# The first quarter of the up projection: half products in a written order, the transposes of h2's last two row tiles at fixed places

## The chip, the cores and the metric

The kernel runs on one core of a Trainium2 chip. The metric is device time in microseconds (us). One execution is also recorded by the hardware profiler, and its trace shows every instruction of every engine: TensorE (PE, and PEld for its weight loads), VectorE (DVE), ScalarE (ACT), GpSimd (POOL) and SyncE (SP), which issues most loads.

## The reference

One decoder block on x of 512 tokens by 1024 features, float32. The change lies where the second half of the block begins:

```python
x = x + (merged @ w_out[l]).astype(x.dtype)
h2 = rmsnorm(x, norm_mlp_g[l])
z = jnp.square(jax.nn.relu(h2 @ w_up[l]))      # 1024 -> 4096
x = x + (z @ w_down[l]).astype(x.dtype)        # 4096 -> 1024
```

Ahead of it stand the input projection, differential attention, pooling and the gates; behind it the final norm.

## The kernel before

**Splitting.** Every float32 operand of a product is split in two parts in a narrower format: a rounded copy made by ACT ("hi") and the remainder made by DVE ("lo"). A product is hi*hi + hi*lo + lo*hi, so three matmuls stand for one. Weights are split by `split_w` (lines 110 to 114: the cast on line 112, the remainder on line 113).

**Seven products instead of eight.** The MLP is cut into four quarters of 1024 hidden features (`for q in range(4): up(q); down(q)`). In `up(q)` the matrix h2 is cut in 2 by 2 blocks (token halves of 256 by feature halves of 512), the weights likewise, and the product is formed with seven block products (a Strassen-like scheme) named by the form of h2 that they use: A11, A12 and A22 are blocks of h2 itself, S1 to S4 are sums and differences of blocks. In the first quarter their order is A11, A12, S1, S2, S3, A22, S4.

**One product** (`product`, lines 749 to 772) has two banks of the accumulation memory (i = 0, 1), and each bank two halves (p = 0, 1) of 256 columns. Such a half product is 12 matmuls of 256 columns: four times hi*hi (line 759) and hi*lo (line 761) in turn, then four times lo*hi (line 764). The two banks are two tiles. S2, S3 and A22 reuse A11's banks, S4 reuses S1's, so they wait until the earlier result has been taken out: by ACT copies (`keep`, line 776) or by DVE sums (`join`, line 780).

**h2 and its transposes** (lines 614 to 646). h2 is made in four row tiles of 128 tokens: DVE scales a row tile (line 623), TensorE transposes it in 2 banks of four 128 x 128 blocks (line 629), and ACT and DVE take the blocks out: for row tiles 0 and 1 as hi and lo of A11 and A12 (lines 641 and 642) and as a plain copy (line 646); for row tiles 2 and 3 as the sums that the S forms need (lines 634 and 635, and `forms_h2`, up to line 603) and as A22's hi and lo. So A11 and A12 need row tiles 0 and 1 alone; S1 is the first that needs row tiles 2 and 3. Row tiles 0 and 2 use accumulation banks 0 and 1, row tiles 1 and 3 use 2 and 3.

**Down** (`down`, line 828 on) takes the seven forms of z; its matmuls (lines 838, 840 and 841) are 512 wide. Its first product in the first quarter uses z's form A11, which is ready before `up` has ended.

**What sets the order.** Each engine runs its own instructions in one fixed order. That order isn't written out in the code: the framework's planner lays it out when the program is built, on a timeline that it simulates. `after(later, earlier)` adds an edge, that "later" is placed behind "earlier"; on one engine this is order alone and adds no wait. Matmuls into one bank keep their order; matmuls into different banks may be laid out in any order that the planner finds. Before the change there were two such edges in the first quarter: the first closing matmul of A11's last half product comes after the very last transpose (lines 765 and 766), and S4's very first matmul after A22's last (lines 768 to 771).

Of the kernel before, what the change touches and what calls it, by code (L numbers as in the profile page):

```python
# [51 lines left out]
def block_kernel(ctx, tc, xT, x_tok, gains, pos, consts, w_in, w_v, w_pool, w_out, w_up, w_dn, out):  # L52
# [4 lines left out]
    def after(later, earlier):  # L57
        tc.add_manual_dep(
            later.ins, earlier.ins.name,
            mybir.DependencyInfo(mybir.DependencyClass.NoSync, mybir.DependencyReason.DATA), reason="issue order",  # L60
        )

    state = {}
# [8 lines left out]
    def bank(i, name):  # L72
        return ps.tile([P, S], F32, tag=f"b{i}", name=name)
# [16 lines left out]
    def f(ap):  # L90
        return ap.bitcast(F32)
# [125 lines left out]
    for n in range(2):  # L217
        accs = [bank((0, 1, 2, 3, 4, 5, 6, 0)[4 * n + t], f"v{n}_{t}") for t in range(NT)]
        for kk in range(4):
# [7 lines left out]
            for k2 in range(2):  # L227
# [4 lines left out]
                k = 2 * kk + k2  # L232
# [11 lines left out]
            if n == 0 and 0 < kk < 3:  # L244
                i = kk - 1
# [287 lines left out]
    A11, A12, A22, A21, S1, S2, S3, S4 = range(8)  # L533
# [44 lines left out]
    def mm_rows(a_, t, k, w, start, stop):  # L578
        hi, lo = w
        sl, tsl = slice((k % 2) * 512, (k % 2) * 512 + 512), slice(t * P, t * P + P)  # L580
        T.matmul(a_, lhsT=mh[:, k, tsl], rhs=hi[:, sl], start=start, stop=False)
        T.matmul(a_, lhsT=mh[:, k, tsl], rhs=lo[:, sl], start=False, stop=False)
        T.matmul(a_, lhsT=ml[:, k, tsl], rhs=hi[:, sl], start=False, stop=stop)

    def x1_add(t, n, a_):
        xs = x1[:, t, n * 512 : n * 512 + 512]
        V.tensor_tensor(out=xs, in0=a_, in1=xs, op=ALU.add)
        square(t, n, R[t][:, 0:2, :].rearrange("p a t -> p (a t)"))
# [29 lines left out]
    for t in range(NT):  # L618
        a_ = bank(4 + t, f"po1_{t}")
        for k in range(NK):  # L620
            mm_rows(a_, t, k, ws[k // 2], k == 0, k == NK - 1)
        x1_add(t, 1, a_)
        V.scalar_tensor_tensor(out=h2[:, t % 2], in0=x1[:, t, :], scalar=row_scale(t, 1), in1=g2b, op0=ALU.mult, op1=ALU.mult)
        pv = []
        for b in range(2):
            pt = bank((t % 2) * 2 + b, f"h2T{t}_{b}")
            for j in range(4):
                k = 4 * b + j
                state["h2T"] = T.transpose(out=pt[:, j * P : j * P + P], in_=h2[:, t % 2, k * P : k * P + P], identity=ident)
            pv.append(pt.rearrange("p (j q) -> p j q", q=P))  # L630
        sl = slice((t % 2) * P, (t % 2) * P + P)
        if t > 1:

            A.copy(out=hw[:, 1, :, sl], in_=pv[0])
            V.tensor_tensor(out=hw[:, 0, :, sl], in0=pv[1], in1=hw[:, 1, :, sl], op=ALU.subtract)
            forms_h2((S1, S2), sl)
        if t == 3:
            forms_h2((S3,), slice(0, HS))
        for b in range(t // 2, 2):
            hi, lo = (gab[b][:, t // 2, i, :, sl] for i in range(2))  # L640
            A.copy(out=hi, in_=pv[b])
            part = V.tensor_tensor(out=lo, in0=pv[b], in1=f(hi), op=ALU.subtract)
            if t == 3:
                after(part, state[S3])
            if t < 2:
                A.copy(out=h2f[:, b, :, sl], in_=pv[b])
# [79 lines left out]
    def bank_view(pa):  # L726
        return [pa[i].rearrange("p (a t) -> p a t", a=2) for i in range(2)]
# [17 lines left out]
    def up(q):  # L745

        W = weights(w_up, q, "u", (A11, A12, S1, S2, S3, A22, S4) if q == 0 else (A11, S1, S2, S3, A22, A12, S4))

        def product(form, name, onto=None):
            w, pa = next(W), onto or [acc(f"u{name}{q}_{i}") for i in range(2)]  # L750
            rh, rl = gf[form]
            first.append(None)
            for i in range(2):
                hi, lo = w[i]
                for p in range(2):
                    a_ = pa[i][:, p * HS : p * HS + HS]
                    for k in range(4):
                        c = slice((p * 4 + k) * P, (p * 4 + k) * P + P)
                        m = T.matmul(a_, lhsT=hi[:, c], rhs=rh[:, k, :], start=p + k == 0 and onto is None, stop=False, skip_group_check=True)  # L759
                        first[-1] = first[-1] or m  # L760
                        T.matmul(a_, lhsT=hi[:, c], rhs=rl[:, k, :], start=False, stop=False, skip_group_check=True)  # L761
                    for k in range(4):
                        c = slice((p * 4 + k) * P, (p * 4 + k) * P + P)
                        m = T.matmul(a_, lhsT=lo[:, c], rhs=rh[:, k, :], start=False, stop=k == 3, skip_group_check=True)  # L764
                        if q == 0 and form == A11 and i + p == 2 and k == 0:
                            after(m, state["h2T"])

            if form == A22:
                state["m4"] = m
            elif form == S4:  # L770
                after(first[-1], state["m4"])
            return pa

        def keep(pa, r):
            for a_, r_ in zip(bank_view(pa), halves(r)):
                A.copy(out=r_, in_=a_)  # L776

        def join(pa, r):
            for a_, r_ in zip(bank_view(pa), halves(r)):
                V.tensor_tensor(out=r_, in0=a_, in1=r_, op=ALU.add)  # L780

        def z_of(r, sign, pa=None):
            for i, r_ in enumerate(halves(r)):
                A.activation(out=r_, in_=bank_view(pa)[i] if pa else r_, func=AF.Relu, scale=sign)
                ins = A.activation(out=r_, in_=r_, func=AF.Square)
            return ins

        ma = product(A11, "m1")
        keep(ma, R[0])
        if q == 0:  # L790
            forms_h2((S4,), slice(0, HS))

        def first_block():
            join(product(A12, "m2"), R[0])
            z_of(R[0], 1.0)
            if q > 0:
                zsplit(q, A11, R[0])

        if q == 0:
            first_block()  # L800
        mc = product(S1, "m5")
        keep(mc, R[2])
        product(S2, "m6", onto=ma)
        keep(ma, R[1])
        product(S3, "m7", onto=ma)
        join(ma, R[2])
        z_of(R[2], -1.0)
        product(A22, "m4", onto=ma)
        if q == 0:
            zsplit(q, A11, R[0])  # L810
        zhi["z21"] = z_of(R[3], 1.0, ma)
        sub(4, 2, 3)
        zsplit(q, S1, R[4])
        if q > 0:
            first_block()
        product(S4, "m3", onto=mc)
        join(mc, R[1])
        z_of(R[1], -1.0)
        zsplit(q, A12, R[1])
        sub(4, 4, 0, neg=True)  # L820
        zsplit(q, S2, R[4])
        sub(1, 4, 1, neg=True)
        zsplit(q, S4, R[1])
        sub(0, 0, 3)
        zsplit(q, S3, R[0])
        zsplit(q, A22, R[2])
# [166 lines left out]
```

## Time and profile before

| | us |
|---|---|
| three runs | 676.32, 676.32, 677.84 |
| median | 676.32 |
| span of the profiled execution, first to last instruction | 675.2 |
| its difference to the median, outside the span | 1.1 |
| TensorE's busy time in that span | 665.3 |
| first matmul of the up projection | 349.82 |
| last closing matmul of S3 begins its group of four | 382.21 |

The profile's times count from the first instruction of the span. A row of the timeline has the start, the length, the engine, the line in the kernel, the operation, the tiles (output, then inputs), the form and how many instructions are merged; in square brackets stands idle time of the engine ahead of it and what ended it. Matmul ends are modelled, so distances are best read from start to start. `um` are the accumulators of the up projection, `dm` those of down; `gab` holds h2's blocks A11, A12 and A22, `gss` the S forms; `wh` and `wl` are the parts of the weights, with the letters u and d for up and down.

### The profile page before, as it was taken

The page shows a single profiled execution, that of the slowest core. Times are in us where ns is not written, and L with a number is a line of the kernel's source. Part 1 is how long each engine was busy: PE and PEld are TensorE (multiplying, and loading weights), DVE is VectorE, ACT ScalarE, POOL GpSimd, SP SyncE. Part 2 cuts the span into 40 slices and gives each one's busy share as a digit, 9 for nine tenths or more (in the row PEclk, how much of TensorE's full clock was granted, in tenths as well). Part 3 has the DMA queues.
Part 4 walks back from the last instruction along what each step waited for, and adds up shares of the span by engine and source line. Part 5 has one row for each costly group of instructions (what it writes and reads, how often), then busy time and mean ns, then how long its engine had stood idle before and what let it go on. Part 6 is the DMA issues. An engine that isn't in the chain of part 4 may idle for free.

```text
span 675.2 us, 9995 instructions
## 1 busy us (share of the span) xinstructions
PE 665.3 (99%) x3686; PEld 579.9 (86%) x3686; DVE 529.1 (78%) x879; ACT 462.5 (68%) x741; POOL 123.0 (18%) x137
## 2 busy tenths in 40 slices
PE   9999999999999999999999999999999999999995
PEld 7788888888888888888889988899889998899884
DVE  6955877799979986975478989667994599747995
ACT  8465587978887698883477975367753696356874
POOL 6201110132133212520201020202103021210120
PEclk9999999999999999999999999999999999999999
DMA  8526574435254364574964678676969579493863
GB/s 272 189 71 182 126 152 125 102 94 126 87 139 105 101 171 94 126 193 177 309 194 79 196 172 241 153 179 155 234 190 197 200 156 260 125 213 131 213 125 124
DMA packets 32880, 109.34 MB, mean 162 GB/s; under 512 B 4032, under 2 KB 4928, under 8 KB 32832
## 3 DMA queue, kind: packets, MB, share of 16 engines
q0 software_dynamic: 10656, 38.80, 32.4%
q1 hardware_dynamic: 21744, 69.38, 29.0%
q8 instruction: 29, 0.48, 0.3%
q10 hardware_dynamic: 432, 0.52, 0.2%
q14 instruction: 19, 0.16, 0.1%
HBM read 106.59 MB, written 2.10 MB: 161 GB/s over the span
## 4 chain that ended last, share of the span: by engine, by line
PE 86%; DMA 5%; issue 5%; DVE 1%; ACT 1%; SPq 0%; DVEq 0%; POOLq 0%
PE dm L838 7%; PE dm L840 7%; PE dm L841 7%; PE um L759 7%; PE um L764 7%; PE um L761 7%; DMA wga_uNone<-w_up 5%; PE o L417 2%; PE ga L132 2%; PE ga L131 2%; PE gp L135 2%; PE k L132 2%; PE gp L132 2%; PE gp L131 2%; PE k L131 2%
## 5 line engine op out<-in xcount | busy, mean ns | idle before, releaser
L840 PE MATMUL dm<-wh_dt,z 128*128 128x512 f32 (+1 forms) x128 | 49.5, 387 | 0.0
L841 PE MATMUL dm<-wl_dt,z 128*128 128x512 f32 (+1 forms) x128 | 49.4, 386 | 0.0
L838 PE MATMUL dm<-wh_dt,z 128*128 128x512 f32 (+1 forms) x128 | 49.0, 387 | 0.0
L759 PE MATMUL um<-gss,wh_ut 128*128 128x256 f32 x192 | 48.1, 284 | 0.1
L761 PE MATMUL um<-gss,wh_ut 128*128 128x256 f32 x192 | 48.1, 283 | 0.0
L400 ACT ACTIVATE p<-p,st 128x128 f32<-128x128 f32 (+3 forms) x64 | 35.8, 560 | 14.1 <-DVE st L396 13.8
L112 ACT CAST wh_ut<-wga_uNone 128x1024 fp32r<-128x1024 f32 x24 | 24.9, 1053 | 28.8 <-PE dm L840 19.2
L856 DVE TENSOR_TENSOR x<-x,dm 128x512 f32<-128x512 f32 x48 | 32.8, 687 | 14.1 <-PE dm L841 14.0
L670 POOL DMA_DIRECT2D wga_dNone<-w_dn x16 | 14.2, 887 | 151.8 <-DVE wl_dt L113 151.8
L113 DVE TENSOR_TENSOR wl_ut<-wga_uNone,wh_ut 128x1024 fp32r<-128x1024 f32 x24 | 29.0, 1224 | 12.5 <-ACT wh_ut L112 12.5
L112 ACT CAST wh_ub<-wr_u 128x1024 fp32r<-128x1024 f32 x24 | 25.1, 1051 | 19.0 <-PE um L761 10.1
L670 POOL DMA_DIRECT2D wga_uNone<-w_up x18 | 15.6, 867 | 120.9 <-DVE wl_ut L113 86.9
L840 PE MATMUL dm<-wh_db,z 128*128 128x512 f32 x96 | 37.2, 389 | 0.0
L841 PE MATMUL dm<-wl_db,z 128*128 128x512 f32 x96 | 37.2, 389 | 0.0
L759 PEld LDWEIGHTS um<-gss,wh_ut 128*128 128x128 f32 x192 | 36.8, 192 | 0.3 <-ACT rawz L776 0.3
L761 PEld LDWEIGHTS um<-gss,wh_ut 128*128 128x128 f32 x192 | 36.9, 192 | 0.0
L838 PE MATMUL dm<-wh_db,z 128*128 128x512 f32 x96 | 35.8, 390 | 0.0
L113 DVE TENSOR_TENSOR wl_ub<-wr_u,wh_ub 128x1024 fp32r<-128x1024 f32 x24 | 29.2, 1222 | 7.9 <-ACT wh_ub L112 7.9
L112 ACT CAST wh_dt<-wga_dNone 128x1024 fp32r<-128x1024 f32 x24 | 24.8, 1050 | 14.6 <-issue 4.1
L735 DVE TENSOR_TENSOR z<-rawz,z 128x1024 fp32r<-128x1024 f32 x28 | 33.7, 1225 | 0.9 <-ACT z L732 0.9
L396 DVE CUSTOM_DVE_ANT_0 p<-s,mask 128x128 f32<-128x128 f32 (+3 forms) x64 | 30.3, 485 | 3.4 <-PE s L395 3.3
L732 ACT CAST z<-rawz 128x1024 fp32r<-128x1024 f32 x28 | 28.7, 1048 | 6.0 <-DVE rawz L741 4.9
(324 smaller groups left out, 2222.9 us busy)
## 6 DMA issues: line engine op xcount, KB each, us to landing
wr_u<-w_up SPq DMA_DIRECT2D x24, 512.0 KB, 5.3
wr_d<-w_dn SPq DMA_DIRECT2D x24, 512.0 KB, 4.2
wga_uNone<-w_up POOLq DMA_DIRECT2D x18, 512.0 KB, 6.7
wga_dNone<-w_dn POOLq DMA_DIRECT2D x16, 512.0 KB, 5.8
wr_k<-w_in SPq DMA_DIRECT2D x8, 512.0 KB, 3.3
wr_ga<-w_in SPq DMA_DIRECT2D x8, 512.0 KB, 3.3
wr_gp<-w_in SPq DMA_DIRECT2D x8, 512.0 KB, 4.2
wl_ga<-w_in POOLq DMA_DIRECT2D x8, 512.0 KB, 5.5
```

Source lines behind the costliest of these rows:

```text
L112: ins = A.copy(out=hi[:, sl], in_=raw[:, sl])
L113: (eng or G).tensor_tensor(out=lo[:, sl], in0=raw[:, sl], in1=f(hi)[:, sl], op=ALU.subtract)
L131: T.matmul(acc, lhsT=hi[:, c], rhs=rh[:, k, :], start=k == 0, stop=False)
L132: T.matmul(acc, lhsT=hi[:, c], rhs=rl[k], start=False, stop=False)
L400: A.activation(out=pr[:, c, :N], in_=pr[:, c, :N], func=AF.Exp, scale=-1.0, bias=st[:, c : c + 1], accum_out=st[:, 2 + c : 3 + c])
L735: V.tensor_tensor(out=z[:, 1], in0=r, in1=f(z[:, 0]), op=ALU.subtract)
L759: m = T.matmul(a_, lhsT=hi[:, c], rhs=rh[:, k, :], start=p + k == 0 and onto is None, stop=False, skip_group_check=True)
L761: T.matmul(a_, lhsT=hi[:, c], rhs=rl[:, k, :], start=False, stop=False, skip_group_check=True)
L764: m = T.matmul(a_, lhsT=lo[:, c], rhs=rh[:, k, :], start=False, stop=k == 3, skip_group_check=True)
L838: m = T.matmul(a_, lhsT=zh, rhs=hi[:, sl], start=p == 0 and start, stop=False, skip_group_check=True)
L840: T.matmul(a_, lhsT=zl, rhs=hi[:, sl], start=False, stop=False, skip_group_check=True)
L841: end = T.matmul(a_, lhsT=zh, rhs=lo[:, sl], start=False, stop=p == 3, skip_group_check=True)
```

## The change

Only the order on TensorE is changed, by edges in the first quarter; no instruction is added or taken away.

- The first transpose of every bank of every row tile is remembered (`state["h2T", t, b]`).
- In the first quarter every half product's first matmul is placed behind the last matmul of the half product before it in program order, through all seven products (`state["um"]`).
- Row tile 2's transposes are placed behind A11's second half product (i = 0, p = 1), row tile 3's behind A12's second half product.
- The edge to the very last transpose moves from A11's last half product to A12's third (i = 1, p = 0).

```diff
             for j in range(4):
                 k = 4 * b + j
+                if j == 1:
+                    state["h2T", t, b] = state["h2T"]
                 state["h2T"] = T.transpose(out=pt[:, j * P : j * P + P], in_=h2[:, t % 2, k * P : k * P + P], identity=ident)
...
                 for p in range(2):
+                    begin = None
                     a_ = pa[i][:, p * HS : p * HS + HS]
...
                         first[-1] = first[-1] or m
+                        begin = begin or m
...
                         m = T.matmul(a_, lhsT=lo[:, c], rhs=rh[:, k, :], start=False, stop=k == 3, skip_group_check=True)
-                        if q == 0 and form == A11 and i + p == 2 and k == 0:
+                        if q == 0 and form == A12 and (i, p, k) == (1, 0, 0):
                             after(m, state["h2T"])
+                    if q == 0:
+                        if (form, i, p) == (A11, 0, 1):
+                            for b in range(2):
+                                after(state["h2T", 2, b], m)
+                        elif (form, i, p) == (A12, 0, 1):
+                            for b in range(2):
+                                after(state["h2T", 3, b], m)
+                        if form != A11 or i + p:
+                            after(begin, state["um"])
+                        state["um"] = m
```

## The prediction

> **What bounds the kernel now.** I read the page first, then the busy time by stretches, then TensorE's timeline in the two stretches that stood out, and last the queues of ScalarE (ACT) and VectorE (DVE) beside them.
>
> ```profile
> span 675.2 us, 9995 instructions
> PE 665.3 (99%) x3686; PEld 579.9 (86%) x3686; DVE 529.1 (78%) x879; ACT 462.5 (68%) x741; POOL 123.0 (18%) x137
> ```
>
> TensorE is the bound. A matmul it doesn't issue in time is paid in full, provided that nothing behind it waits anyway. The stretches show where that holds (columns: length, then the busy time of PE, PEld, DVE, ACT, POOL, and the granted clock):
>
> ```profile
> 349.80:351.80 2.00, 1.42 (x8) 0.90 (x8) 2.00 (x5) 1.61 (x4) 0.00 (x0) 1.00 0.98 387
> 351.80:364.40 12.60, 12.60 (x108) 12.60 (x107) 10.76 (x16) 9.58 (x19) 1.73 (x2) 1.00 0.30 57
> 364.40:378.70 14.30, 14.30 (x121) 14.30 (x120) 12.59 (x13) 12.85 (x17) 1.73 (x2) 1.00 0.84 193
> 378.70:379.75 1.05, 0.64 (x4) 0.24 (x3) 1.05 (x2) 1.05 (x3) 0.00 (x0) 1.00 0.90 339
> 379.75:388.30 8.55, 8.55 (x71) 8.55 (x72) 8.55 (x9) 7.08 (x10) 0.00 (x0) 1.00 0.36 120
> 388.30:426.90 38.60, 38.60 (x195) 32.77 (x194) 35.95 (x37) 24.35 (x28) 5.25 (x6) 1.00 0.74 187
> 426.90:666.00 239.10, 239.10 (x1534) 218.80 (x1533) 183.69 (x202) 149.70 (x191) 33.26 (x38) 1.00 0.72 181
> ```
>
> From 351.80 us to the last matmuls TensorE stands still once, near 379 us. The quarter that is changed (349.8 to about 396 us) has two holes, and behind it lie 239.10 us without one. So whatever the change gains or loses in this quarter goes one to one into the time, as long as nothing new goes wrong behind it. The holes, by starts, since the ends of matmuls are modelled:
>
> ```profile
> 349.82 0.87 PE L759 MATMUL um<-gab,wh_ub 128*128 128x256 f32 x3
> 351.28 0.66 PE L629 MATMUL h2T<-ident,h 128*128 128x128 f32 x4 [0.58 <-ACT h2f L646]
> 351.80 0.39 PE L761 MATMUL um<-gab,wh_ub 128*128 128x256 f32 x1
> 352.02 0.28 PE L759 MATMUL um<-gab,wh_ub 128*128 128x256 f32 x1
> 352.14 0.28 PE L761 MATMUL um<-gab,wh_ub 128*128 128x256 f32 x1
> 359.89 1.03 PE L629 MATMUL h2T<-ident,h 128*128 128x128 f32 x8
> 360.69 0.96 PE L764 MATMUL um<-gab,wl_ub 128*128 128x256 f32 x6
> 364.35 0.40 PE L759 MATMUL um<-gss,wh_ut 128*128 128x256 f32 x2
> ...
> 378.39 0.52 PE L764 MATMUL um<-gss,wl_ut 128*128 128x256 f32 x3
> 379.24 0.38 PE L759 MATMUL um<-gss,wh_ub 128*128 128x256 f32 x1 [0.32 <-ACT gss L602]
> 379.71 0.39 PE L759 MATMUL um<-gss,wh_ut 128*128 128x256 f32 x1
> ```
>
> In the stream a 256-wide matmul starts every 0.12 us (352.02 to 352.14), so a half product of 12 is 1.44 us. Eight transposes hold TensorE from 359.89 to 360.69, some 0.10 us each. Just after a hole the first matmul takes 0.22 us instead of 0.12 (351.80 to 352.02), so a hole costs 0.10 us on top.
>
> **First hole, A11's beginning.** The three L759 at 349.82 are first matmuls of three banks: a half product alternates L759 and L761, and three L759 in a row can't be of one. A11's next matmul is the L761 at 351.80, which multiplies by the remainder of h2's first two row tiles. Who makes that remainder:
>
> ```profile
> 348.66 1.28 DVE L623 SCALAR_TENSOR_TENSOR h<-x,st,rawz 128x1024 f32<-128x1024 f32 x1
> 349.86 1.88 DVE L642 TENSOR_TENSOR gab<-h2T,gab 128x512 fp32r<-128x512 f32 x3
> 355.91 1.28 DVE L623 SCALAR_TENSOR_TENSOR h<-x,st,rawz 128x1024 f32<-128x1024 f32 x1
> 361.18 0.69 DVE L635 TENSOR_TENSOR hw<-h2T,hw 128x512 f32<-128x512 f32 x1
> 362.58 0.69 DVE L603 TENSOR_TENSOR gss<-hw,gss 128x512 fp32r<-128x512 f32 x1
> ```
>
> The third L642 ends at 349.86 + 1.88 = 351.74, and the L761 starts 0.06 us later. Program order of lines 638 to 642 makes that third one row tile 1's first bank, which A11 needs. So A11 waits for DVE until 351.80 whatever TensorE's order is. Before, two first matmuls of other banks (2 x 0.12) and the four transposes of row tile 2's first bank (4 x 0.10, from 351.28) were done inside this wait. The change holds the first matmul of each half behind the last of the half ahead, and row tile 2's transposes behind A11's second half. Nothing else of TensorE's is ready then, so this cover is gone: 0.24 + 0.40 = **+0.64 us**. Bounds: nothing, if DVE takes the remainders ahead of the 1.28 us of scaling row tile 2 (which is less urgent now, but was ready first); nor can it cost more, since the wait's end is DVE's.
>
> A rule of the Trainium skill bears on this ("TensorE: Matmul & The Clock Gate", Part 2, Step-by-step): weight loads may be pulled ahead, but the matmuls stay in program order. In the trace nothing passes the transposes that wait until 351.28, which agrees. By that rule a written order turns each late operand into a hole; if matmuls could pass each other, this term would be nothing and the sum below 0.64 us lower.
>
> **Row tiles 2 and 3.** No transpose is added. Row tile 2 goes behind A11's second half, which costs only what stands above. Row tile 3's eight stood behind all of A11 and A12's first bank except 6 closing matmuls (the x6 at 360.69), and stand now behind all of that: 6 x 0.12 = 0.72 us later, and with the 0.64 us they start at about 361.3 instead of 359.9. Behind them wait ACT L634 (in the fence below), DVE L635 and the two steps of S1's form, ending with DVE L603 at 362.58 + 0.69 = 363.27. That moves to about 364.6. S1 started at 364.35 and would now start at 364.35 + 0.64 = 365.0. So 0.4 us of margin is left: cost nothing. If DVE puts one weight remainder of 1.22 us (L113's size, below) ahead of it, it is 0.8 us late, and with the 0.10 that makes 0.9 us: the upper bound.
>
> **Second hole, the middle of S3.** After the last of S3's first bank (378.39 + 3 x 0.12 = 378.75) came a first matmul of S4, taken ahead of its turn, at 379.24, and S3's second bank only at 379.71. ACT's queue beside it:
>
> ```profile
> 360.53 0.59 ACT L634 COPY hw<-h2T 128x512 f32<-128x512 f32 x1 [1.48 <-PE h2T L629]
> 375.04 2.24 ACT L112 CAST wh_ut<-wga_uNone 128x1024 fp32r<-128x1024 f32 x2
> 377.18 1.05 ACT L112 CAST wh_ub<-wr_u 128x1024 fp32r<-128x1024 f32 x1
> 378.14 1.04 ACT L602 CAST gss<-hw 128x1024 fp32r<-128x1024 f32 x1
> 379.09 0.57 ACT L776 COPY rawz<-um 128x512 f32<-128x512 f32 x1
> ```
>
> The S4 matmul waited for L602 (ends 379.18), S3's second bank for L776, the copy that frees its bank, which ends at 379.66. The chain forbids the S4 matmul there (it opens S4's second bank), but that alone frees nothing: the copy is ACT's. Lost before: 0.96 us less the 0.12 of useful work, plus 0.10: 0.94 us. After, TensorE comes to this place 0.64 us later, at 379.39. If ACT's queue stands as it is, 379.71 - 379.39 + 0.10 = 0.42 us is still lost, a saving of **0.52 us**. If ACT runs earlier by 0.3 us (row tile 2's copies leave a place ahead of the S1 casts), the whole 0.94 us is saved; if ACT is late by as much as TensorE, nothing. I take the rows as they stand.
>
> **A22 and S4.** S4's second bank ran between A22's two banks and can't any more:
>
> ```profile
> 382.69 0.28 PE L759 MATMUL um<-gab,wh_ut 128*128 128x256 f32 x1
> 385.57 0.28 PE L761 MATMUL um<-gss,wh_ub 128*128 128x256 f32 x1
> 388.33 0.40 PE L838 MATMUL dm<-wh_db,z 128*128 128x512 f32 x1
> 388.56 0.40 PE L840 MATMUL dm<-wh_db,z 128*128 128x512 f32 x1
> ...
> 384.68 1.22 DVE L113 TENSOR_TENSOR wl_db<-wr_d,wh_db 128x1024 fp32r<-128x1024 f32 x1
> 385.81 0.69 DVE L780 TENSOR_TENSOR rawz<-um,rawz 128x512 f32<-128x512 f32 x1
> 386.42 1.22 DVE L700 TENSOR_TENSOR wga_dNone<-wr_d,wal_d 128x1024 f32<-128x1024 f32 x1
> ```
>
> A22's first bank ends at 385.57. Its second needs the join L780, which frees the bank at 385.81 + 0.69 = 386.50. In between only the down projection's first product is free. Its matmuls take 0.23 us (388.33 to 388.56); the first that needs a weight remainder is the third, at 385.57 + 0.46 = 386.03, and that remainder (L113) is done at 385.90. Before, the planner put down matmuls in this very place while A22 waited (388.33), so I take them as the cover: cost **nothing**. Without it A22 starts at about 386.55: 0.98 + 0.10 = 1.08 us. Below nothing it can't go, for this place had no hole.
>
> **The sum.** 0.64 - 0.52 = +0.12 us on a span of 675.2. The median of the runs shown, 676.32, lies 1.1 us over this execution's span; the same 1.1 us gives 675.2 + 0.12 + 1.1 = 676.4. What the measurement of this kernel tells from no change is about 0.3%, 2.0 us. The sum lies far inside it, and so do most of its bounds: -0.30 with ACT early, up to 0.12 + 0.9 + 1.08 = 2.1 with S1 late and A22 uncovered.
>
> **Rivals.**
>
> *Slower: A22 locked behind its join.* The place is 385.57 us. With S4 behind the chain, TensorE has only the down projection's matmuls there. DVE has no idle time in that stretch (8.55 of 8.55), and the planner lays its queue out anew. If two of the 1.22 us instructions slip ahead of L780, each taking 1.13 us of the queue (384.68 to 385.81), the join ends at 386.50 + 2.26 = 388.8. Without down matmuls in between, TensorE waits 3.2 us + 0.10, and the sum is +3.4: 679.7. It decides the sign once the uncovered wait passes 1.8 us, so from a join that ends after 387.4. Against it: the down product's first half was ready in just that place. For it: S4's second bank was the main cover before, 2.76 us of it (385.57 to 388.33), and it is gone. Chance 0.10.
>
> *Faster: both holes close.* DVE takes the remainders ahead of L623, A11 starts 1.2 us earlier and TensorE stands 0.6 us instead of 1.9; and ACT's copy comes early enough for S3. Then the first term becomes 0.64 - 1.2 = -0.56 and the second -0.94: -1.5, 674.8, still inside 0.3%. Only with a further gain behind it (the last hole's remainder, 0.6 us) does it reach -2.1: 674.2. Against it: L623's input was there first, and nothing of the change reaches DVE before 351 us. Chance of passing 2.0 us: 0.05.
>
> *The reshuffle.* The planner may change the order of ACT, DVE and the loads all through the later quarters. They have no hole now (239.10 of 239.10), so a new order can only leave that so or cost something. Casts of 1.05 us and remainders of 1.22 us are the units: one late costs about 1 us (677.4), two or more pass the bound. Chance of one 0.15, of passing the bound 0.03.
>
> *It does nothing.* The order changes only inside waits for DVE and ACT, so time stays: 676.3. This is inside the forecast's own range.
>
> **How the numbers follow.** The forecast with its own bounds has 0.67: 675.9 to 677.4 (with one of the two upper terms at most). With the one-late-cast case (677.4, 0.15) that makes 0.82 inside 675.4 to 678.0, which I give as the range: half a microsecond wider than these cases on each side, for the spread of the runs' median. Faster by over 0.3%: 0.05. Slower by over 0.3%: 0.10 + 0.03 = 0.13. Within: 0.82.
>
> **What would show it.** Right: in the changed profile TensorE has a hole of about 1.9 us behind A11's first matmul, ended by DVE L642, with no transpose in it; eight transposes in one row after 24 and after 72 matmuls of A11 and A12; no S4 matmul before A22's last; a hole of 0 to 0.4 us in the middle of S3, ended by ACT L776; down matmuls between A22's two banks. Wrong: A11's second matmul earlier than DVE's third L642 before it, a hole over 1.8 us at A22's second bank, S1 waiting for DVE L603, or new holes after the first quarter.

## The result and the profile after

The kernel after takes 679.27 us in the median (677.35 to 681.41, 16 executions), the kernel before 676.81 (676.02 to 678.71, 16 executions) beside it: a ratio of 1.0034 [1.0026, 1.0042]. The change makes the kernel slower by 2.5 us, a little more than the 0.3% that was given as the bound (which lies inside the interval). The forecast was 676.4, and its range ended at 678.0.

The page of the kernel after, the two rows that answer to those of before:

```profile
span 675.0 us, 9994 instructions
PE 664.4 (98%) x3686; PEld 580.0 (86%) x3686; DVE 528.9 (78%) x879; ACT 461.1 (68%) x741; POOL 122.7 (18%) x137
```

This span is no longer than that of before (675.2). So the span of one execution doesn't show the loss. The profiled execution of after took 677.35 us, the lowest of its 16. The loss has to be looked for in the stretches, and in the other executions. The busy time by stretches, kernel after (columns as in the prediction):

```profile
349.16:351.12 1.96, 0.39 (x3) 0.19 (x2) 1.96 (x5) 1.59 (x4) 0.00 (x0) 1.00 1.01 393
351.12:363.64 12.52, 12.52 (x106) 12.52 (x107) 9.69 (x15) 9.21 (x19) 1.72 (x2) 1.00 0.48 90
363.64:378.00 14.36, 14.36 (x122) 14.36 (x121) 13.93 (x15) 13.41 (x19) 1.73 (x2) 1.00 0.69 171
378.00:384.50 6.50, 6.50 (x56) 6.45 (x54) 6.50 (x7) 5.10 (x8) 0.00 (x0) 1.00 0.35 125
384.50:385.32 0.82, 0.16 (x3) 0.01 (x1) 0.82 (x3) 0.82 (x2) 0.00 (x0) 1.00 0.00 0
385.32:394.00 8.68, 8.68 (x72) 8.68 (x73) 8.25 (x8) 7.25 (x12) 3.51 (x4) 1.00 0.79 189
426.70:665.90 239.20, 239.20 (x1535) 218.87 (x1534) 182.60 (x200) 149.55 (x191) 33.18 (x38) 1.00 0.72 180
```

There are two holes, as before, but the second has moved: the stretch around 379 us is filled (6.50 of 6.50), and a new hole stands at 384.50 to 385.32. The later quarters are full, as before. TensorE's timeline of the kernel after at these places:

```profile
349.16 0.39 PE L762 MATMUL um<-gab,wh_ub 128*128 128x256 f32 x1
351.12 0.38 PE L765 MATMUL um<-gab,wh_ub 128*128 128x256 f32 x1 [1.57 <-DVE gab L644]
...
353.98 1.04 PE L631 MATMUL h2T<-ident,h 128*128 128x128 f32 x8
360.60 1.03 PE L631 MATMUL h2T<-ident,h 128*128 128x128 f32 x8
364.34 0.28 PE L762 MATMUL um<-gss,wh_ut 128*128 128x256 f32 x1
...
378.74 0.28 PE L762 MATMUL um<-gss,wh_ut 128*128 128x256 f32 x1
...
384.02 0.64 PE L768 MATMUL um<-gab,wl_ut 128*128 128x256 f32 x4
385.32 0.39 PE L762 MATMUL um<-gab,wh_ut 128*128 128x256 f32 x1 [0.66 <-DVE rawz L794]
...
394.06 0.40 PE L852 MATMUL dm<-wh_db,z 128*128 128x512 f32 x1
426.72 0.28 PE L762 MATMUL um<-gab,wh_ub 128*128 128x256 f32 x1
```

(L762, L765 and L768 were L759, L761 and L764 before, L631 was L629, L644 was L642, L790 was L776, L794 was L780, L798 was L784.) From A11's first matmul to the second quarter's first I count what I call *the quarter*: 426.72 - 349.16 = 77.56 us. Before it was 426.87 - 349.82 = 77.05, by this row of the kernel before:

```profile
426.87 0.28 PE L759 MATMUL um<-gab,wh_ub 128*128 128x256 f32 x1
```

From there to the last matmul the traces have 240.85 us before and 240.86 after. A11 itself starts 0.66 us earlier in the trace of after, and that hides the longer quarter in the span. This start scatters: over the traces of all the kernels below it lies between 348.75 and 350.84 us; why isn't shown. VectorE's and ScalarE's timeline of the kernel after, beside the holes:

```profile
349.18 1.88 DVE L644 TENSOR_TENSOR gab<-h2T,gab 128x512 fp32r<-128x512 f32 x3
383.44 1.22 DVE L113 TENSOR_TENSOR wl_db<-wr_d,wh_db 128x1024 fp32r<-128x1024 f32 x1
384.57 0.69 DVE L794 TENSOR_TENSOR rawz<-um,rawz 128x512 f32<-128x512 f32 x1
...
376.98 1.04 ACT L602 CAST gss<-hw 128x1024 fp32r<-128x1024 f32 x1
377.93 0.57 ACT L790 COPY rawz<-um 128x512 f32<-128x512 f32 x1
...
385.17 0.59 ACT L798 ACTIVATE rawz<-um 128x512 f32<-128x512 f32 x1
```

A11's hole ends with DVE's third L644 (349.18 + 1.88 = 351.06). S3's hole is gone because ACT's copy of S2's second bank, L790, ends at 378.50, ahead of the first matmul that needs the bank, at 378.74. A22's second bank waits until the join L794 has ended (385.26), and the down projection's matmuls, which were to fill this wait, begin only at 394.06, behind all of S4. As ACT's queue stands they couldn't have filled it: in the kernel's code the accumulation banks go round (`acc`, line 649 of the kernel before: 4, 5, 6, 7, 0, 1), and down's first product gets the two banks of A22. ACT reads A22's first bank out until 385.76 (L798), half a microsecond behind the join. In the kernel before it was so too: this row ends at 386.83, and the join had ended at 386.50.

```profile
386.24 0.59 ACT L784 ACTIVATE rawz<-um 128x512 f32<-128x512 f32 x1
```

The other part is outside the span, in the time of an execution less its span. All 111 executions of the kernel before whose span is on record have 1.80 to 1.99 us there. The kernel after has 2.4 in the mean of its 16. And the list of granted clocks has a third part: no execution of before is under 0.996, while 7 of the 16 of after are at 0.994 or 0.995. These seven have a mean span of 677.7 us, the other nine of 676.1.

### The profile page after: what moved, and what is told of

The parts are those of the page before. It is cut to its first block, busy times and chain, and to the rows that moved or that the text cites. A ratio compares the mean times of both kernels' runs of the same rounds, so it can differ in the third digit from the quotient of the medians.

```text
span 675.0 us, 9994 instructions
## 1 busy us (share of the span) xinstructions
PE 664.4 (98%) x3686; PEld 580.0 (86%) x3686; DVE 528.9 (78%) x879; ACT 461.1 (68%) x741; POOL 122.7 (18%) x137
## 4 chain that ended last, share of the span: by engine, by line
PE 96%; DVE 2%; issue 1%; ACT 0%; POOL 0%; DVEq 0%; POOLq 0%
PE dm L852 7%; PE dm L854 7%; PE dm L855 7%; PE um L765 7%; PE um L762 7%; PE um L768 7%; PE v L235 2%; PE o L417 2%; PE ga L132 2%; PE ga L131 2%; PE gp L135 2%; PE gp L132 2%; PE k L132 2%; PE k L131 2%; PE gp L131 2%; PE k L135 2%
## 5 line engine op out<-in xcount | busy, mean ns | idle before, releaser
L762 PE MATMUL um<-gss,wh_ut 128*128 128x256 f32 x192 | 48.1, 283 | 0.0
L765 PE MATMUL um<-gss,wh_ut 128*128 128x256 f32 x192 | 48.1, 283 | 0.0
L762 PEld LDWEIGHTS um<-gss,wh_ut 128*128 128x128 f32 x192 | 36.9, 192 | 0.0
L765 PEld LDWEIGHTS um<-gss,wh_ut 128*128 128x128 f32 x192 | 36.9, 192 | 0.0
L765 PE MATMUL um<-gab,wh_ub 128*128 128x256 f32 x128 | 32.5, 283 | 1.6 <-DVE gab L644 1.6
```

## The experiments

Two theories stood at the start. *The holes*: the loss lies in the quarter, in A11's hole and in A22's, which the order opened. *Elsewhere*: the quarter costs little, and the loss comes from the executions around it (the clock, the time outside the span). Both turned out to hold a part, and the parts don't add up to the whole.

| kernel | median us (executions) | ratio to before | quarter | outside the span |
|---|---|---|---|---|
| before, again | 677.14 (12) | 0.9997 [0.9988, 1.0007] | 77.18 | 1.9 |
| after, again | 679.20 (8) | 1.0033 [1.0019, 1.0047] | 78.06 | 2.3 |
| e_nochain | 678.74 (11) | 1.0029 [1.0017, 1.0041] | 77.80 | 2.4 |
| e_latechain | 679.07 (5) | 1.0032 [1.0020, 1.0044] | 78.40 | 2.4 |
| e_t2free | 680.17 (6) | 1.0046 [1.0030, 1.0061] | 79.00 | 2.4 |
| e_keepfirst | 675.83 (11) | 0.9983 [0.9974, 0.9992] | 76.45 | 1.9 |
| e_fill12 | 678.35 (12) | 1.0019 [1.0009, 1.0030] | 78.30 | 2.4 |
| e_wide2 | 682.41 (4) | 1.0085 [1.0067, 1.0102] | 81.58 | 2.15 |
| e_wide_mm | 680.49 (3) | 1.0050 [1.0031, 1.0068] | 80.61 | 2.2 |
| e_wide_tr | 681.51 (2) | 1.0066 [1.0041, 1.0091] | 81.11 | 2.2 |
| e_act2 | 679.28 (9) | 1.0035 [1.0023, 1.0046] | 79.28 | 1.9 |
| e_act2fill | 678.29 (12) | 1.0022 [1.0013, 1.0031] | 77.82 | 1.9 |
| e_s4free | 676.24 (12) | 0.9990 [0.9980, 1.0001] | 76.63 | 1.85 |
| e_s4fill | 676.49 (11) | 1.0003 [0.9994, 1.0012] | 76.67 | 1.9 |
| e_best1 | 675.60 (11) | 0.9986 [0.9977, 0.9996] | 75.98 | 1.9 |

The quarter is that of one profiled execution, from A11's first matmul to the second quarter's first.

**Both kernels again.**

> The kernel before, run as it is, to read span and granted clock of each of its executions. Theory C (the clock: the hole of 1.9 us that the change opens behind the transposes lets the granted TensorE clock fall to half for some microseconds in most executions, and the profiled execution of the changed kernel was one that escaped): clock 0.997 to 0.998 in nearly all executions, time about 676.8, spans about 674.4, that is 2.4 us under the times as in the changed kernel. Theory D (no clock: loads or waits in later quarters that differ from execution to execution): its clocks scatter as the changed kernel's do, 0.994 to 0.998.

> The changed kernel again. Both theories: about 679.2, ratio 1.0034. C: granted clock 0.994 to 0.996 in more than half of its executions, and these are the slower ones, by about 2 us against those at 0.998; if the profiled execution is one of them, the trace shows a stretch of some 4 to 5 us at half clock between 347 and 356 us with matmuls every 0.24 us. D: no such stretch; holes behind 396 us.

The times came out as before. The clock did not do what was expected of it: one of the eight executions of after is under 0.996, not more than half, and three with 0.997 or 0.998 still take 679.7 to 681.2 us. So the median of after, 679.27 with seven low clocks in 16 and 679.20 with one in eight, doesn't hang on the clock alone. In the second trace of after, A11's hole is longer (its second matmul at 351.81, 1.90 us of idle time ahead of it), which makes its quarter 78.06. So the quarter costs 77.56 - 77.05 = 0.5 us in one pair of traces and 78.06 - 77.18 = 0.9 in the other.

**Parts of the order alone.** First the transposes' places without the chain of half products, then the chain from S1 on with A11, A12 and the transposes as in the kernel before, then all but row tile 2's place.

```diff
e_nochain, against the kernel after
-                        if form != A11 or i + p:
-                            after(begin, state["um"])
e_latechain, against the kernel after
-                        if q == 0 and form == A12 and (i, p, k) == (1, 0, 0):
+                        if q == 0 and form == A11 and i + p == 2 and k == 0:
...
-                        if (form, i, p) == (A11, 0, 1):
-                            for b in range(2):
-                                after(state["h2T", 2, b], m)
-                        elif (form, i, p) == (A12, 0, 1):
-                            for b in range(2):
-                                after(state["h2T", 3, b], m)
-                        if form != A11 or i + p:
+                        if form not in (A11, A12):
e_t2free, against the kernel after
-                        if (form, i, p) == (A11, 0, 1):
-                            for b in range(2):
-                                after(state["h2T", 2, b], m)
-                        elif (form, i, p) == (A12, 0, 1):
+                        if (form, i, p) == (A12, 0, 1):
```

> The changed kernel without the chain: the two rows of transposes stay at their fixed places, but the first matmul of a half product may go ahead of its turn again. So far the traces give three parts of the loss: the quarter itself (77.6 and 78.1 us from A11's first matmul to the second quarter's first, against 77.1 and 77.2), 0.5 us outside the span, and, in a part of the executions, a granted clock of 0.994 to 0.995 instead of 0.996 to 0.998, which would be one 3.4 us window at half clock (1.7 us). Theory A (the chain costs it: S4's second bank can't cover A22's wait for its join): no hole at A22, the quarter 76.2 to 76.7 us, time 676.3 to 677.3. Theory B (row tile 2's late transposes cost it, by the hole at A11's beginning and what that does to the clock): A11's hole still 1.6 us or more, some executions at 0.995 and below, time 678 or more.

> The other part alone: A11, A12 and all transposes as before the change, the chain from S1 on. A: S3's hole stays near 0.9 us (ACT's copy is as late as before, and the S4 matmul is gone from it) and A22 has a hole of 0.9 us: quarter 77.9 to 78.2 us, time 677.8 to 678.3, clock 0.996 to 0.998 in all executions. B: 676.8 to 677.2.

> The changed kernel without the edge that puts row tile 2's transposes behind A11's second half product; the chain of half products and row tile 3's place stay. The first four transposes fall back into the wait at A11's beginning. By the prediction's own sum: 0.4 us less than the changed kernel. C: the transposes count little as work for the clock, so something between 677.5 and 679.0, with clocks between. D: 678.8, clocks as the changed kernel.

None of the three brings the time of before back, and two miss what was expected: e_latechain is 0.8 us over the range of its theory A, and e_t2free, expected 0.4 us under the kernel after, is 0.9 over it. Each has holes of its own. One row of each kernel's TensorE timeline, first e_nochain:

```profile
366.61 0.38 PE L765 MATMUL um<-gss,wh_ut 128*128 128x256 f32 x1 [1.15 <-DVE gss L603]
```

e_latechain:

```profile
379.30 0.39 PE L762 MATMUL um<-gss,wh_ut 128*128 128x256 f32 x1 [0.58 <-ACT rawz L784]
386.49 0.50 PE L846 MATMUL dm<-wh_db,z 128*128 128x512 f32 x1 [1.18 <-ACT rawz L792]
```

and e_t2free:

```profile
351.19 0.66 PE L631 MATMUL h2T<-ident,h 128*128 128x128 f32 x4 [1.10 <-ACT h2f L648]
379.84 0.39 PE L762 MATMUL um<-gss,wh_ut 128*128 128x256 f32 x1 [0.44 <-ACT rawz L787]
383.30 0.39 PE L762 MATMUL um<-gab,wh_ut 128*128 128x256 f32 x1 [0.33 <-DVE rawz L791]
```

The idle time in brackets is less than the loss, since ends are modelled: by starts e_t2free loses 1.4, 0.6 and 0.5 us at these rows, and another 1.0 at A22's second bank. In e_latechain the planner did lay down matmuls into A22's wait (the second row), and the first of them waits itself, for ACT's L792, which reads A22's first bank out: 1.3 us by starts. Without the chain S1 is late behind DVE's L603, which the prediction had as a bound (0.9 us): here it is 1.3 us by starts. The holes of these kernels differ in place and length, with ACT's and DVE's queues laid out anew for each.

**One wait of the kernel before, mended by itself.** ACT's cast for S4 (L602) stood ahead of its copy of S2's second bank (L776), and S3 waited for the copy.

```diff
e_keepfirst, against the kernel before
-            A.copy(out=hi, in_=u if form == S3 else w)
+            state["cast", form] = A.copy(out=hi, in_=u if form == S3 else w)
...
-                A.copy(out=r_, in_=a_)
+                ins = A.copy(out=r_, in_=a_)
+            return ins
...
-        keep(ma, R[1])
+        kept = keep(ma, R[1])
+        if q == 0:
+            after(state["cast", S4], kept)
```

> The kernel before with one edge on ACT instead of the change: the cast of S4's form comes behind the copy that frees S3's second bank. If S3's hole before (0.94 us) is ACT's order alone, TensorE finds the bank free: hole under 0.2 us, quarter 76.2 us, time about 0.9 us under before (676.0 to 676.3). If something else is late there (weights, the form S3), the hole stays and the time is 676.9 to 677.1.

The quarter fell by 0.6 to 0.7 us, the time by 1.2. One edge on ACT takes most of S3's hole away (0.38 us by starts are left) without an order on TensorE.

**The hole and the clock.** Twelve copies of A11's first matmul fill A11's hole; they go into A11's second bank, which A11's own first matmul there clears later. Then the hole is made wider: DVE makes the remainder of row tile 1's first bank three times.

```diff
e_fill12, against the kernel after
-                        T.matmul(a_, lhsT=hi[:, c], rhs=rl[:, k, :], start=False, stop=False, skip_group_check=True)
+                        if q == 0 and (form, i, p, k) == (A11, 0, 0, 0):
+                            for _ in range(12):
+                                fill = T.matmul(pa[1][:, :HS], lhsT=hi[:, c], rhs=rh[:, k, :], start=True, stop=True, skip_group_check=True)
+                                after(fill, m)
+                                m = fill
+                        rest = T.matmul(a_, lhsT=hi[:, c], rhs=rl[:, k, :], start=False, stop=False, skip_group_check=True)
+                        if q == 0 and (form, i, p, k) == (A11, 0, 0, 0):
+                            after(rest, m)
e_wide2, against the kernel after
-            part = V.tensor_tensor(out=lo, in0=pv[b], in1=f(hi), op=ALU.subtract)
+            for _ in range(3 if (t, b) == (1, 0) else 1):
+                part = V.tensor_tensor(out=lo, in0=pv[b], in1=f(hi), op=ALU.subtract)
e_wide_mm: both, with range(32) for range(12)
e_wide_tr: as e_wide_mm, with range(36), and
-                                fill = T.matmul(pa[1][:, :HS], lhsT=hi[:, c], rhs=rh[:, k, :], start=True, stop=True, skip_group_check=True)
+                                fill = T.transpose(out=pa[1][:, :P], in_=ident, identity=ident)
```

> The changed kernel with the hole at A11's beginning filled: 12 copies of A11's first matmul are written to the accumulation bank of A11's second half, which that half clears when it starts, and stand between A11's first and second matmul (12 x 0.12 = 1.44 us of the 1.9 us wait). Nothing waits less. C: the clock stays at 0.997 to 0.998 and the time falls by about 2 us, to 677.0 to 677.5, though work is added. D, and a theory that the waits themselves cost the time: 679.2, as the changed kernel.

> The changed kernel with the hole at A11's beginning made wider: DVE computes the remainder that A11 waits for three times, and two of its other instructions get ahead of the last. The hole grows from 1.9 to about 4 us. If the wait is all, the time grows by the added wait, 2 us, to 681.3 at most (less if S3's and A22's waits shrink), with clocks as in the changed kernel. If an idle TensorE lets its clock fall, nearly every execution shows it: 0.993 to 0.995, a stretch of 3.4 us at half clock behind the hole with a matmul every 0.24 us, and 1 to 1.7 us more: 682 to 683.

> The kernel e_wide2 (DVE's remainder of row tile 1's first bank done three times, which widened A11's hole to 4.35 us, and behind which the clock record showed 0.5 for 3.413 us) with that hole filled by 32 copies of A11's first matmul, 32 x 0.12 = 3.8 us, into A11's second bank, which A11 clears when it comes to it. Theory A (it is TensorE's idle time in the hole that halves the clock): no record of 0.5 behind the hole, granted clock 0.996 or more in all executions, and a time some 1.5 us below e_wide2's 682.4, about 681. Theory B (the half clock comes of something else that the longer work of DVE does): the record of 0.5 stays, the clock stays at 0.995 or less and the time at 682.4.

> As the kernel with 32 matmuls in the widened hole, but with 36 transposes of the 128x128 identity in it instead, 36 x 0.109 = 3.9 us, on the same bank. TensorE is as busy as with the matmuls. Theory A (transposes keep the clock as matmuls do): no record of 0.5, clock 0.996 or more, time about 681. Theory B (transposes count for less than matmuls, and the window of the clock sees a hole): the record of 0.5 stays behind the transposes, the clock is 0.995 or less, and the time about 682.4. Theory B would also say why a hole of 1.9 us, with sixteen transposes ahead of it, is enough in a third of the executions of the kernel after.

With the hole filled none of 12 executions of e_fill12 has a clock under 0.996, and the median is 0.9 us less (about 2 were expected), though its quarter in the profile (78.30) is no shorter. Not all of the 0.9 can be the clock's: the executions of after with 0.996 or more have a mean span of 676.5 us (16 in the two series), those of e_fill12 676.0. With the hole widened to 4.35 us all four executions are at 0.993 to 0.995, and the trace shows why. Stretches of e_wide2, cut where its clock record changes:

```profile
350.56:353.98 3.41, 0.10 (x1) 0.11 (x1) 3.37 (x7) 2.74 (x9) 0.00 (x0) 1.00 0.31 126
353.98:357.39 3.41, 3.41 (x17) 3.41 (x18) 3.34 (x5) 2.18 (x3) 0.39 (x1) 0.50 0.00 0
357.39:360.80 3.41, 3.41 (x31) 3.41 (x31) 1.13 (x2) 1.61 (x4) 1.34 (x2) 1.00 0.67 100
```

Behind 3.41 us in which TensorE did almost nothing (0.10 us) come 3.41 us at a granted clock of 0.50, with 17 matmuls instead of 31, and then the full clock again. With the hole filled, by matmuls (e_wide_mm, clock 0.997 to 0.998) or by transposes (e_wide_tr, 0.996 to 0.997), there is no such window. So it is TensorE's idle time that halves the clock, and transposes in its place keep the clock up as matmuls do. Whether they count for as much isn't measured.

Does the change's own hole, of some 2 us, do it? The profile of e_act2 (below), with the hole of the kernel after, is of such an execution. Its stretches, cut in the same way (TensorE alone):

```profile
349.90:353.32 3.41, 1.63 (x11) 1.00 0.74 298
353.32:356.73 3.41, 3.41 (x18) 0.50 0.00 0
356.73:360.14 3.41, 3.41 (x31) 1.00 0.28 36
```

and its timeline of TensorE:

```profile
350.13 0.39 PE L765 MATMUL um<-gab,wh_ub 128*128 128x256 f32 x1
352.30 0.39 PE L768 MATMUL um<-gab,wh_ub 128*128 128x256 f32 x1 [1.78 <-DVE gab L647]
...
354.03 0.41 PE L765 MATMUL um<-gab,wh_ub 128*128 128x256 f32 x1
354.25 0.41 PE L768 MATMUL um<-gab,wh_ub 128*128 128x256 f32 x1
```

The matmuls start 0.21 us apart (354.03 to 354.25) instead of 0.12. Sixteen at 0.093 us too much make 1.5 us, about the difference of the mean spans of after (677.7 against 676.1). The window ahead was busy for 1.63 us of 3.41. In the two traces of after, cut at the same multiples of 3.413 us from their own clock record, the hole lies in windows that are busy for a little longer. The kernel after:

```profile
347.91:351.32 3.41, 1.84 (x13) 1.33 (x12) 3.34 (x5) 3.04 (x7) 0.00 (x0) 1.00 0.82 288
351.32:354.74 3.41, 3.41 (x30) 3.41 (x30) 2.02 (x5) 3.34 (x9) 0.00 (x0) 1.00 0.05 22
```

The kernel after, again:

```profile
348.21:351.62 3.41, 1.70 (x12) 1.19 (x10) 3.28 (x7) 2.73 (x6) 0.00 (x0) 1.00 0.69 239
351.62:355.03 3.41, 3.22 (x27) 3.23 (x28) 2.01 (x6) 3.33 (x9) 0.00 (x0) 1.00 0.18 71
```

Neither is followed by half the clock. In all 17 traces, cut in this way between 10 and 660 us, the windows of e_wide2 and e_act2 are the only ones that are busy for under 1.70 us, and the only ones with half the clock behind them. So what decides seems to be how the hole falls into a window: it begins 1.37 us into one in the first trace of after, 1.43 in the second and 0.35 in e_act2. The Trainium skill ("TensorE: Matmul & The Clock Gate", Part 1, What's actually happening) says that the activity window is free-running and 3413 ns long. The records agree with the length: those at the full clock last a multiple of it (e_act2: 102 and 93 windows), and the hole's three places fit a free-running window. It gives as a rule (the same page, HAM oscillation — how this bites in real kernels) that gaps over some 3.4 us are to be avoided; here 2.05 us by starts (350.25 to 352.30) were enough, so the measurement decides for a smaller figure. In the kernels with this hole (after twice, e_act2, e_s4free) 14 of 45 executions are at 0.995 or less.

**Outside the span.** The traces of the kernels with 1.9 us outside the span have 952 or 953 rows of ACT (before: 741 busy ones and 211 of its sequencer), those with 2.3 to 2.4 have 950 or 951 (the three wide ones, at 2.15 to 2.2, have 951 and two more rows of DVE).

```diff
e_act2, against the kernel after
+    spare = cp.tile([P, 2], F32, name="spare")
+    for i in range(2):
+        A.copy(out=spare[:, i : i + 1], in_=ident[:, i : i + 1])
e_act2fill: e_act2 and e_fill12 together
```

> The kernel after with two more tiny copies on ACT (128x1 each) at the very start; nothing else is edited. Question: the executions of the kernel before take 1.80 to 1.98 us more than their span, those of the kernel after mostly 2.3 to 2.56, and the kernels with the smaller figure are those with 211 or 212 ACT instructions in the trace, the others have 209 or 210. Theory A (the part outside the span goes with the number of ACT's instructions): time less span falls to about 1.87, and the median falls by about 0.5, to 678.7 where the kernel after has 679.2. Theory B (it goes with something else of the change, such as how the end of the program falls): time less span stays at 2.3 to 2.5 and the median at about 679.3.

> The kernel after with both the two tiny ACT copies at the start and the 12 copies of A11's first matmul in A11's hole: of the three places found (the quarter, the part outside the span, the half clock behind the hole) only the quarter is left. Theory A (the three add up, and there is nothing else): time less span 1.87, granted clock 0.996 or more in every execution, the quarter 77.6 to 78.3 us, and a median 0.7 to 1.1 above the kernel before, 677.7 to 678.1. Theory B (part of the loss is somewhere else): the median stays at 678.4 or more.

Two copies of 128x1 more, 953 rows of ACT: 8 of 9 executions of e_act2 have 1.82 to 1.90 us outside the span (one 2.33), and all 12 of e_act2fill 1.83 to 1.91. So this half microsecond does go with the count of ACT's rows, and not with the order on TensorE alone; e_s4free and e_best1, with 952 and 953, have the smaller figure too. What in the count makes it isn't shown. The median of e_act2 did not fall, a miss: five of its nine executions have a clock of 0.995, more than the kernel after has, and its A11 starts later in the profile (350.13). Nor does e_act2fill gain anything over e_fill12, where no clock is low in either: it has 0.5 us less outside the span, 0.6 us more in the span (676.6 against 676.0 in the mean), and the same median (678.29 and 678.35). So it isn't shown that the half microsecond costs time. The two copies may only move it into the span.

In e_act2fill only the quarter should be left, 0.7 to 1.1 us. Measured are 678.29 - 676.8 = 1.5. So the account of three places does not close: some 0.4 to 0.8 us of the executions' time remain unplaced.

**The order without S4.** S4 alone is let out of the chain; then the same with the hole filled; then a version put together from what the runs showed.

```diff
e_s4free, against the kernel after
-                        if form != A11 or i + p:
+                        if form != S4 and (form != A11 or i + p):
e_s4fill: e_s4free and e_fill12 together
e_best1: e_latechain with
-                        if form not in (A11, A12):
+                        if form not in (A11, A12, S4):
and the edge of e_keepfirst
```

> The kernel after, with the fixed order taken from S4's two half products alone: A11, A12, S1, S2, A22, A21 and S3 keep it, S4 may go where its operands are there. Theory A (A22's second bank stands behind its join and S4's second bank isn't let past, so TensorE stands 0.82 us): S4's second bank goes into A22's place as in the kernel before, the hole at the end of A22 closes, the quarter comes to about 76.7 us instead of 77.6 to 78.1, and the time falls by about 0.9, to 678.3. Theory B (the hole's time is taken up by another wait, such as S4 then meeting the end of its own operands or the down products coming late): the hole is gone but the quarter stays above 77.3, and the time within 0.3 of the kernel after.

> The kernel after without the order on S4 and with the 12 copies of A11's first matmul in the hole. The quarter should be that of the kernel without the order on S4, 76.6 us, or up to 0.5 more where the copies hold a half product up. Theory A (the executions of that kernel at 677.5 and 678.0 with a clock of 0.997 and 0.995 are half clock behind the hole): no execution with 0.995 or less, the median at 676.2 and the highest below 677.3. Theory B (these executions are scatter of the early transfers): one or two in twelve stay above 677.3.

> A version put together from what the runs showed: A11, A12 and the transposes as in the kernel before (no order among them), the fixed order from S1 on but not on S4, and ACT's cast for S4 behind its copy that keeps S2's second bank. Theory A (holes are worth their length): A11's hole 0.8 to 1.0, S3's 0 to 0.4, none at A22, a quarter of about 76.1 us, no half clock, 1.87 outside the span, and a median of about 675.5, at or below the 675.83 of the kernel before with that one ACT edge. Theory B (S4's parts that run early leave a hole later, or ACT is late for S1): a quarter of 76.6 or more and a median at 676.0 or above.

TensorE's timeline of e_s4free:

```profile
348.75 0.38 PE L762 MATMUL um<-gab,wh_ub 128*128 128x256 f32 x1
350.71 0.38 PE L765 MATMUL um<-gab,wh_ub 128*128 128x256 f32 x1 [1.57 <-DVE gab L644]
...
383.59 0.64 PE L768 MATMUL um<-gss,wl_ub 128*128 128x256 f32 x4
384.07 0.28 PE L762 MATMUL um<-gab,wh_ut 128*128 128x256 f32 x1
```

S4's second bank went ahead of A22 as a whole, a little earlier than in the kernel before: its last four matmuls start at 383.59, and A22's first bank follows without a wait. So A22 comes 23 matmuls (2.8 us) later, when the join is done, and its second bank has no wait either. A22's hole is gone, A11's stays, and the quarter is 425.38 - 348.75 = 76.63, as expected. The time fell by 3.0 us, not by 0.9, and so the whole loss against the kernel before is gone (0.9990 [0.9980, 1.0001]). The quarter gives 0.9 to 1.4 of it, the part outside the span 0.5 by the sum (ACT has 952 rows again), and the clock perhaps 0.4: one execution in 12 is at 0.995, with the same hole in A11, and 8 in 24 of the kernel after. The rest isn't placed. In e_s4fill none is under 0.996, but three of eleven still take 678.2 to 678.9: that scatter isn't the clock's.

e_best1 keeps what each part was good for, and its timeline has one hole, covered as in the kernel before by two early first matmuls and four transposes:

```profile
349.27 0.87 PE L762 MATMUL um<-gab,wh_ub 128*128 128x256 f32 x3
350.71 0.66 PE L631 MATMUL h2T<-ident,h 128*128 128x128 f32 x4 [0.56 <-ACT h2f L648]
351.23 0.38 PE L765 MATMUL um<-gab,wh_ub 128*128 128x256 f32 x1
...
425.25 0.28 PE L762 MATMUL um<-gab,wh_ub 128*128 128x256 f32 x1
```

The quarter is 425.25 - 349.27 = 75.98 us (76.1 expected), no execution is under 0.996, and at 675.60 it beats the kernel before and the kernel after, like e_keepfirst.

## Why the prediction was wrong, point by point

- **A11's hole, +0.64: right.** The hole has 1.84 us by starts and 0.10 behind it, ended by DVE's third L644, with no transpose in it. Before, the same place lost 1.98 - 0.36 - 0.40 + 0.10 = 1.32 (three matmuls and four transposes were done in it). That is +0.62, with the mechanism that was given.
- **Row tile 3 later, nothing: right for this kernel.** The eight transposes stand at 353.98 and 360.60, behind 24 and 72 matmuls as forecast, and S1 begins at 364.34 without a wait. The bound behind it was real: e_nochain shows S1 waiting for L603, 1.3 us.
- **S3's hole, -0.52: mis-sized.** It measured -0.94, the other bound of the prediction: ACT's copy ended 378.50 - 349.16 = 29.34 us behind A11's first matmul instead of 379.66 - 349.82 = 29.84. With the 0.64 us by which TensorE comes later this closes the whole hole.
- **A22's second bank, nothing: this step failed.** The prediction took down matmuls as cover, because before the planner had put some into this very place "while A22 waited". That misread the row: at 388.33 the join (ended at 386.50) had long freed A22's second bank, so they covered no wait. And down matmuls were not free to start in it, as the prediction had them. Their first bank is A22's first, and ACT had read that out only at 386.83 before and 385.76 after, behind the join both times (386.50 and 385.26); e_latechain shows a down matmul waiting for it. After, they all stand behind S4, from 394.06. The hole has 0.82 us and 0.10 behind it, +0.92, near the bound of 1.08 that the prediction gave. The slower rival had the place and the cause right (A22 behind its join, S4 no longer in between), with a price of 3.4 us that a later join would have made; the join came without that delay. e_s4free shows it: with S4 let out, the hole is gone.
- **The sum.** 0.62 - 0.94 + 0.92 = +0.60 for the quarter, measured 0.5 and 0.9, forecast 0.12.
- **1.1 us outside the span: wrong.** That was the shown median less the profiled span, as though the profiled execution were a median one. The time outside the span is 1.8 to 2.0 us in every execution of before, so the profiled one stood near 677.0. The base of the sum, 676.32, was the median of three runs; 16 gave 676.81. And this part isn't fixed: after the change it is 0.5 larger.
- **The clock: missing.** The stretches showed a granted clock of 1.00 everywhere, and I weighed no case in which it changes. With a hole made longer from 1.10 to 1.84 us by starts, 7 of 16 executions, and 1 of 8 in the second series, have the low clock of half a window lost, 1.5 us each.
- **Later quarters unchanged: right** (240.85 and 240.86 us from the second quarter's first matmul to the last).

Of the 2.5 us, the quarter is 0.5 to 0.9 by the two pairs of traces. The part outside the span is 0.5, and whether that costs time isn't shown. The clock is 8/24 of 1.5 = 0.5 in the mean of both series. That leaves 0.6 to 1.0 open. Without the eight executions of low clock, the mean span of after is 676.5 us against 675.25 before: of this 1.25 the quarter's 0.5 to 0.9 leaves 0.4 to 0.8 unplaced as well. A11's hole differs from execution to execution (1.57 and 1.90 us of idle time in two traces), and both traces of after come from fast executions (677.35, the lowest of 16; 678.28, the second lowest of 8), so the quarter may be longer in the others; no run shows it.

## What to carry to other kernels

A written order on one engine turns every late operand into a hole, so ask of each place where two independent streams were mixed what filled the wait, and count as cover only what the new order still lets stand there and what has its operands and its bank by then. Here an edge that frees a late producer (ACT's copy ahead of its cast) gained 1.2 us, and fixing the consumer's order lost 2.5. Compare stretches by their own landmarks, and read the whole list of executions with clock and span: one profiled execution can be the fastest of its kernel.

## What the runs showed of the hardware

- A hole of 2.05 us, shorter than a window of 3.413 us, had half of TensorE's clock behind it for the next window (e_act2): windows busy for 0.10 and 1.63 us were followed by 0.50, windows busy for 1.70 and 1.84 us were not. These are four windows, and how the activity is counted isn't shown.
- In a hole of some 4 us, 36 transposes of 128x128 kept the clock (0.996 and 0.997 in two executions), as 32 matmuls 256 wide did (0.997 to 0.998 in three).
- At the clock of 0.50 a 256-wide matmul starts every 0.21 us instead of 0.12.
- Half a microsecond outside the span went with the count of ACT's instructions (950 or 951 against 952 or more in the trace), and two copies of 128x1 took it away, without a shorter time.
